# Feed-forward weights and residual of a hybrid decoder trunk: the fourth block split on the engines, output tiles added to the residual in DRAM by transfer

## The chip, the cores and the metric

The kernel runs on one core of one Trainium2 chip. The metric is the device time of one execution in microseconds (us), and the time of a kernel is the median of its runs. The engines are named as in the profile: PE (TensorE's matmuls), PEld (its weight loads), DVE (VectorE), ACT (ScalarE), POOL (GpSimd) and SP (SyncE). GpSimd and SyncE do hardly anything here but issue transfers. A transfer issued on SyncE goes into one DMA queue, one issued on GpSimd into another; both are served by the same 16 DMA engines.

## The reference

A trunk of two layers, all in float32, with 512 tokens, a model width of 1024 and a hidden width of 2816. Each layer has a mixing part and a feed-forward part. Only the second one is touched:

```python
for i in range(DEPTH):                      # DEPTH = 2
    h = rmsnorm(x, norm_mix[i])
    ...
    x = x + merged @ w_mix_o[i]             # attention, convolution and state-space branches, gated
    h = rmsnorm(x, norm_ffn[i])
    gt, up = jnp.split(h @ w_ffn_in[i], 2, axis=-1)
    x = x + (jax.nn.silu(gt) * up) @ w_ffn_out[i]
return rmsnorm(x, norm_final)
```

## The kernel before

**Products of split numbers.** Data are kept transposed: 128 channels on the partitions, 512 tokens along the free axis, so that the residual is eight tiles of 128x512. TensorE multiplies in a reduced format, fp32r. Every operand is therefore kept as two tiles, hi (the value rounded to fp32r) and lo (what is left over, rounded too), and a product is three matmuls, hi by hi, hi by lo and lo by hi (`mm3`, L271; all its matmuls are at L275). Making a pair costs one copy on ScalarE for hi and one subtraction on VectorE for lo (`lo_of`, L189, whose instruction is at L190).

**The feed-forward part.** The hidden width is 22 tiles of 128, taken in five groups: tiles 0 to 5, 6 to 9, 10 to 13, 14 to 17 and 18 to 21. Tiles 0 to 5 are computed plainly. A tile from 6 on is a "pair tile": its gate and its up projection are treated as the two rows of a 2x2 block matrix and multiplied in seven products instead of eight (`seven_products`, L1130). Each product runs over four blocks of the inner width, with three 128x256 matmuls for each, so a pair tile has 84 matmuls. The seven products are gathered in the PSUM tiles pb, pc and pd; ScalarE copies parts of them into the SBUF tiles ga and ub in between (L1148 to L1155), and VectorE later finishes ga by adding pd (L1168 in a pair tile, L1187 in an output; all such additions are recorded at L363) and ub from pb (recorded at L367). This finishing is deferred: it is a generator that runs beside the products of the next tile. In a pair tile a Silu on ScalarE follows (L1169).

The output of the groups 6 to 9, 10 to 13 and 14 to 17 is made in seven products too (`out_pairs`, L1177, called in the loop below after the first pair tile of the group that follows). It goes through the eight residual tiles two by two, four steps of 42 matmuls, and adds each result onto the residual, which at that time lies in DRAM as `xkept`: for each tile, 128x512 numbers or 256 KB, SyncE loads the old value into a tile xs (L1184), VectorE adds ga or ub, and SyncE stores xs back (L1189 and L1193). So there are three such output groups in a layer, with eight loads and eight stores each. The loads of a step are issued one step ahead. After the last pair tile the residual is loaded once more (xres, L1250), and the last group's output, `pfo`, is added to it in SBUF.

**Weights of the pairs.** Every pair tile, and every two steps of an output group, takes one item of weights from a DRAM tensor `wsp`; there are 22 items in a layer. `fetch_chunk` (L168) issues an item's transfers on GpSimd's queue: r2 plainly (L175, 128x1024, 512 KB), h4 (L176, 128x512, 256 KB), a second block accumulated onto r2 (L177), and r1 (L178). An accumulating transfer reads what lies at its destination and writes the sum back. h4 is the fourth block of the matrix, which the transfer itself rounds to fp32r. `item_steps` (L201) then makes the seven operands: ScalarE writes -h4 into l4 (L195) and GpSimd issues a transfer that accumulates the block onto it (L196), which leaves the block's low part; h1 is copied from r1, r3 is added up from r2 and r1 on VectorE (L225 and L227), and h2, l1, h3, l2, l3 follow in this order. `feed`, called after each of the seven products, advances this by two steps. Two items are fetched ahead.

**Buffers and order.** r1, r2 and r3 share 5 buffers (NPART), the hi tiles of 128x1024 share 5, the lo tiles 5, and all tiles of 128x512 (xs, ga, ub, h4, l4, the operands) share 58. Each engine works its instructions off in one fixed order. That order is chosen when the kernel is built, by a scheduler that models durations, except in one part of the kernel's beginning that is ordered by hand. The same holds for GpSimd's and SyncE's lists of transfers: a transfer that has to wait for a buffer or a result holds up all that stand behind it in that list.

Of the kernel before, what the change touches and what calls it, by code (L numbers as in the profile page):

```python
# [9 lines left out]
F32 = mybir.dt.float32  # L10
F32R = mybir.dt.float32r
I32 = mybir.dt.int32
AF = mybir.ActivationFunctionType
ALU = mybir.AluOpType
PSUM = bass.MemoryType.PSUM

P = 128
D = 1024
S = 512
DEPTH = 2  # L20
KT = D // P
# [59 lines left out]
def hybrid_kernel(ctx, tc, xin, wst, wsp, vec, ssp, ssb, sbt, cst, out):  # L81
    nc = tc.nc
    V, A, T = nc.vector, nc.scalar, nc.tensor
# [13 lines left out]
    def u2(shape, dt=F32, name="u2"):  # L97
        return up.tile(shape, dt, tag="u2", bufs=NU2, name=name)
# [58 lines left out]
    raws = []  # L157

    def wraw(name, dt=F32):
        return wp.tile([P, 1024], dt, tag="part", bufs=NPART, name=name)  # L160

    def whi(name="whi", dt=F32R):
        return wp.tile([P, 1024], dt, tag="whi", bufs=NHI, name=name)

    def wlo(name="wlo", dt=F32R):
        return wp.tile([P, 1024], dt, tag="wlo", bufs=NLO, name=name)

    def fetch_chunk(queue=nc.sync, parts=1):  # L168
        i, n, *half = items[loaded[0]]
        loaded[0] += 1  # L170
        if n is None:

            r1, r2, h4 = wraw("r1"), wraw("r2"), u2([P, S], F32R, "h4")
            n = half[0]
            nc.gpsimd.dma_start(r2[:, : 2 * n], wsp[i, :, 1024 : 1024 + 2 * n])  # L175
            nc.gpsimd.dma_start(h4[:, :n], wsp[i, :, 2048 : 2048 + n])  # L176
            nc.gpsimd.dma_start(r2[:, : 2 * n], wsp[i, :, 2048 : 2048 + 2 * n], accum_op=ALU.add)  # L177
            nc.gpsimd.dma_start(r1[:, : 2 * n], wsp[i, :, 0 : 2 * n])  # L178
            raws.append((i, n, r1, r2, h4))
            return None  # L180
        raw = wp.tile([P, 1024], F32, tag="raw", bufs=NRAW, name="raw")
        n //= parts
        cuts = [slice(j * n, (j + 1) * n) for j in range(parts)]
        for c in cuts:
            dma = queue.dma_start(raw[:, c], wst[i, :, c])
        raws.append((raw, cuts))
        return dma

    def lo_of(lo, raw, hi):  # L189
        V.tensor_tensor(out=lo, in0=raw, in1=hi.bitcast(F32), op=ALU.subtract)  # L190
        return lo

    def rest_of(lo, hi, src):

        A.activation(lo, hi.bitcast(F32), AF.Copy, scale=-1.0)  # L195
        nc.gpsimd.dma_start(lo, src, accum_op=ALU.add)  # L196
        return lo

    fetched = [0]
# [1 line left out]
    def item_steps():  # L201
        if not raws:
            fetch_chunk()
        got = raws.pop(0)
        while sum(1 + (len(x) > 3) for x in raws) < fetched[0] and loaded[0] < len(items):
            fetch_chunk()
        if len(got) == 2:
            raw, cuts = got
            hi, lo = whi(), wlo()
            for c in cuts:  # L210
                A.copy(hi[:, c], raw[:, c])  # L211
                yield
                lo_of(lo[:, c], raw[:, c], hi[:, c])
                yield
            ready.append((cuts[-1].stop * 3 // P, (hi, lo)))
            return
        i, n, r1, r2, h4 = got
        a, b, ab = slice(0, n), slice(n, 2 * n), slice(0, 2 * n)
        l4 = u2([P, S], F32R, "l4")
        rest_of(l4[:, a], h4[:, a], wsp[i, :, 2048 : 2048 + n])  # L220
        yield
        h1 = whi("h1")
        A.copy(h1[:, ab], r1[:, ab])
        r3 = wraw("r3")
        V.tensor_tensor(out=r3[:, a], in0=r2[:, a], in1=r1[:, a], op=ALU.add)  # L225
        yield
        V.tensor_tensor(out=r3[:, b], in0=r3[:, a], in1=r1[:, b], op=ALU.add)  # L227
        yield
        h2, l1 = whi("h2"), wlo("l1")
        A.copy(h2[:, ab], r2[:, ab])  # L230
        lo_of(l1[:, ab], r1[:, ab], h1[:, ab])
        yield
        h3, l2 = whi("h3"), wlo("l2")
        A.copy(h3[:, ab], r3[:, ab])  # L234
        lo_of(l2[:, ab], r2[:, ab], h2[:, ab])
        yield
        l3 = wlo("l3")
        lo_of(l3[:, ab], r3[:, ab], h3[:, ab])
        part = lambda h, l, c: (h[:, c], l[:, c])
        ready.append((7 * n // P * 3 // 2,  # L240
            dict(a11=part(h1, l1, a), a12=part(h1, l1, b), s1=part(h2, l2, a), s3=part(h2, l2, b),
                 s2=part(h3, l3, a), s4=part(h3, l3, b), a22=part(h4, l4, a))
        ))
        yield

    def load_chunk():
        for _ in item_steps():
            pass
# [3 lines left out]
    def feed(steps=1000):  # L252

        while steps and sum(n for n, _ in ready) < AHEAD and (feeding or raws or loaded[0] < len(items)):
            if not feeding:
                feeding.append(item_steps())
            if next(feeding[0], "end") == "end":
                feeding.pop()
            steps -= 1

    def take():
        while not ready:
            feed(1)
        return ready.pop(0)[1]
# [97 lines left out]
    def tt(out, a, b, op):  # L362
        V.tensor_tensor(out=out, in0=a, in1=b, op=op)  # L363
        return out

    def stt(out, a, s, b, o0, o1):
        V.scalar_tensor_tensor(out=out, in0=a, scalar=s, in1=b, op0=o0, op1=o1)  # L367
        return out
# [10 lines left out]
    for k in range(KT):  # L379
# [3 lines left out]
        if k == 3:  # L383
            fetch_chunk()
    xg = []
    first = item_steps()
    with tc.manual_schedule(engines={mybir.EngineType.DVE, mybir.EngineType.Activation}):
        for k in range(KT):
# [63 lines left out]
    def first_products(ssum):  # L452

        u = u_products(ssum)
        pq, ws = [mmps([P, S], "pqb") for _ in range(NB - 1)], [chunk()]
        q_products(pq, ws, [0], range(NB - 1))
        u = u_evacuated(*u)
        ws.append(chunk())
        q_products(pq, ws, [1], range(NB - 1))
        pq.append(mmps([P, S], "pqb"))  # L460
        q_products(pq, ws, [0, 1], [NB - 1])
        return u + ((pq, ws),)
# [5 lines left out]
    uts, rcol, rb, r2, qprod = first_products(ssum)  # L468
# [16 lines left out]
    def tiny(dt=F32, shape=(P, LQ)):  # L485
        _n[0] += 1
        return cp.tile(list(shape), dt, name=f"ssm_c{_n[0]}")
# [73 lines left out]
    for lo_, hi_, by in ((2, 3, 1), (3, 5, 2)):  # L561
        n = hi_ - lo_
        dst = [pw[:, i, lo_:hi_] for i in range(2)]
        src = [pw[:, i, lo_ - by : hi_ - by] for i in range(2)]
        m = [pw[:, i, by : by + 1].to_broadcast([P, n, LQ]) for i in range(2)]
# [27 lines left out]
    r4 = er  # L593
    for _ in range(2):
        cph, sph = double_angle(cph, sph)
        r4 = tt(tiny(), r4, r4, ALU.mult)
# [324 lines left out]
    for l in range(DEPTH):  # L921
        if l > 0:
            uts, rcol, rb, r2, qprod = first_products(ssum)
# [204 lines left out]
        flat = lambda x: x.rearrange("p a c -> p (a c)")  # L1128
# [34 lines left out]
        def pair_tile(made, beside):  # L1163

            ga, ub, pd, pb = seven_products(ops, beside, take())

            def evacuated():
                tt(ga, ga, pd, ALU.add)  # L1168
                A.activation(ga, ga, AF.Silu)  # L1169
                yield  # L1170
                stt(ub, pb, -1.0, ub, ALU.mult, ALU.subtract)
                yield
                yield from made(flat(ga), flat(ub))

            return [evacuated()]

        def out_pairs(ops, beside):  # L1177

            xs = []

            def fetch_x(m):
                xs.append([u2([P, S], F32, "xs") for _ in range(2)])
                for j in range(2):
                    nc.sync.dma_start(xs[-1][j], xkept[:, m + j])  # L1184

            def evacuated(m, x, ga, ub, pd, pb):
                tt(ga, ga, pd, ALU.add)  # L1187
                tt(x[0], x[0], flat(ga), ALU.add)
                nc.sync.dma_start(xkept[:, m], x[0])  # L1189
                yield  # L1190
                stt(ub, pb, -1.0, ub, ALU.mult, ALU.subtract)
                tt(x[1], x[1], flat(ub), ALU.add)
                nc.sync.dma_start(xkept[:, m + 1], x[1])  # L1193
                yield

            fetch_x(0)
            for m in range(0, KT, 2):
                if m + 2 < KT:
                    fetch_x(m + 2)
                if m % 4 == 0:  # L1200
                    w = take()
                got = seven_products(ops, beside, w, m % 4)
                beside = [evacuated(m, xs.pop(0), *got)]
            return beside

        xkept = dr.tile([P, KT, S], F32, name=f"xkept{l}")
        nonlocal_rb = []
        beside, due = [], []
        for gi, (f0, f1) in enumerate(FGROUPS):
# [14 lines left out]
            for f in range(f0, f1):  # L1224
# [12 lines left out]
                beside = pair_tile(made, beside)  # L1237
                if due:
                    beside = out_pairs(due.pop(), beside)
# [6 lines left out]
            beside = []  # L1246
# [238 lines left out]
```

## Time and profile before

| | |
|---|---|
| median of 3 runs | 1584.59 us (1581.96 to 1584.94) |
| profiled execution | 1581.27 us, its span 1579.3 us |
| granted TensorE clock, mean over the span | 0.994 |

Busy time of the engines in the four stages of the program (PE, PEld, DVE, ACT and POOL with their instruction counts, then the granted clock, the DMA engines' mean busy share and GB/s):

```profile
0.00:503.00 503.00, 494.74 (x2467) 406.55 (x2468) 374.62 (x894) 211.63 (x387) 61.73 (x122) 1.00 0.38 117
503.00:800.00 297.00, 291.52 (x2150) 278.36 (x2150) 228.03 (x309) 164.05 (x279) 70.53 (x104) 1.00 0.85 235
800.00:1277.00 477.00, 475.57 (x2391) 390.80 (x2390) 342.75 (x750) 197.28 (x366) 60.43 (x116) 1.00 0.36 108
1277.00:1579.30 302.30, 283.03 (x2201) 275.44 (x2199) 227.30 (x342) 158.10 (x283) 75.41 (x111) 0.97 0.79 217
```

The first and the third stage are the mixing parts and the plain tiles of the two layers. The second and the fourth hold the pair tiles and the output groups, and the fourth also the end of the program. The DMA engines work more than twice as hard in the second and fourth stage as in the others. The transfers that the change touches are these (queue, count, size of one, median us from its issue to its landing):

```profile
r<-wsp POOLq DMA_DIRECT2D x132, 512.0 KB, 6.5
...
xs<-xkept SPq DMA_DIRECT2D x48, 256.0 KB, 6.1
xkept<-xs SPq DMA_DIRECT2D x48, 256.0 KB, 6.4
h<-wsp POOLq DMA_DIRECT2D x44, 256.0 KB, 5.8
l<-wsp POOLq DMA_DIRECT2D x44, 256.0 KB, 7.3
```

A row of a timeline gives the start in us, the duration, engine, line, operation, output and inputs with their shapes, a count, and in brackets how long the engine sat idle before it and what ended that. A row of the list of waits gives the waiting tile, what it waited for, the total, how often, and the longest.

### The profile page before, as it was taken

To read this page: it belongs to the slowest core of one execution; us is meant where nothing else is said; L and a number is where in the kernel's file an instruction comes from. 1 tells how busy PE (TensorE), PEld (TensorE's weight loads), DVE (VectorE), ACT (ScalarE), POOL (GpSimd) and SP (SyncE) were. 2 spreads that over 40 slices of the span, in tenths; PEclk is the share of its full clock that TensorE was granted. 3 is DMA by queue.
4 is the path that set the end of the run, shared out by engine and by line. 5 is a ranking of instruction groups with operands and counts; after the bars stand their busy time and mean duration, and the time that the engine had idled before them with its cause. 6 is when DMAs were issued, how large, how long until landed. Compare 5 with 4: busy or idle time off the path is not lost.

```text
span 1579.3 us, 24934 instructions
## 1 busy us (share of the span) xinstructions
PE 1544.9 (98%) x9204; PEld 1351.1 (86%) x9204; DVE 1172.7 (74%) x2294; ACT 731.1 (46%) x1314; POOL 268.1 (17%) x451
## 2 busy tenths in 40 slices
PE   9899999999999999999999999999999999999996
PEld 7777878888888999999888778788888889999995
DVE  7985869766667687988768666896476756888876
ACT  4345533334444365665524555233444434665652
POOL 0301023210001133332020012122100012333201
PEclk9999999999999999999999999999999999999998
DMA  6423235432533899989543233345234258999952
GB/s 224 124 82 81 78 94 136 137 107 89 179 100 96 227 223 273 280 235 255 188 140 114 74 84 89 115 111 157 73 126 160 84 161 215 252 253 287 271 166 89
DMA packets 108026, 245.89 MB, mean 156 GB/s; under 512 B 23072, under 2 KB 28480, under 8 KB 107904
## 3 DMA queue, kind: packets, MB, share of 16 engines
q1 hardware_dynamic: 69280, 144.77, 28.0%
q0 software_dynamic: 38336, 99.00, 25.7%
q8 instruction: 73, 1.20, 0.3%
q10 hardware_dynamic: 288, 0.52, 0.1%
q14 instruction: 49, 0.40, 0.1%
HBM read 218.01 MB, written 22.02 MB: 152 GB/s over the span
## 4 chain that ended last, share of the span: by engine, by line
PE 82%; DMA 6%; DVE 5%; issue 4%; ACT 1%; POOL 1%; SPq 0%; DVEq 0%; POOLq 0%; ACTq 0%
PE pg L275 17%; PE pc L275 11%; PE py L275 8%; PE pd L275 7%; PE pfo L275 7%; PE pb L275 7%; PE px L275 6%; PE pfu L275 4%; PE pfg L275 4%; DMA r<-wsp 3%; DMA xkept<-xs 2%; PE pu L275 1%; PE pqb L275 1%; PE pz L275 1%; PE pS L857 1%
## 5 line engine op out<-in xcount | busy, mean ns | idle before, releaser
L211 ACT CAST whi<-raw 128x1024 fp32r<-128x1024 f32 (+2 forms) x214 | 195.4, 917 | 434.2 <-PE pg L275 114.2
L190 DVE TENSOR_TENSOR wlo<-raw,whi 128x1024 fp32r<-128x1024 f32 (+2 forms) x214 | 225.4, 1055 | 93.9 <-ACT whi L211 82.3
L190 DVE TENSOR_TENSOR l<-r,h 128x1024 fp32r<-128x1024 f32 x132 | 160.4, 1218 | 12.5 <-ACT h L234 10.5
L275 PE MATMUL pg<-hi,whi 128*128 128x512 f32 x384 | 152.2, 396 | 0.0
L275 PE MATMUL pg<-hi,wlo 128*128 128x512 f32 x384 | 150.4, 392 | 0.0
L275 PE MATMUL pg<-lo,whi 128*128 128x512 f32 x384 | 150.0, 391 | 0.0
L275 PE MATMUL pd<-hi,l 128*128 128x256 f32 x528 | 148.1, 283 | 1.7 <-DVE l L190 1.7
L275 PE MATMUL pd<-hi,h 128*128 128x256 f32 x528 | 148.3, 283 | 0.0
L275 PE MATMUL pd<-lo,h 128*128 128x256 f32 x528 | 147.9, 283 | 0.0
L275 PE MATMUL pb<-hi,h 128*128 128x256 f32 x352 | 100.5, 285 | 6.9 <-ACT ga L1148 5.5
L275 PEld LDWEIGHTS pd<-hi,l 128*128 128x128 f32 x528 | 100.9, 192 | 2.1 <-DVE l L190 2.1
L275 PEld LDWEIGHTS pd<-lo,h 128*128 128x128 f32 x528 | 100.9, 192 | 0.0
L275 PEld LDWEIGHTS pd<-hi,h 128*128 128x128 f32 x528 | 100.9, 192 | 0.0
L275 PE MATMUL pb<-hi,l 128*128 128x256 f32 x352 | 99.6, 283 | 0.0
L275 PE MATMUL pb<-lo,h 128*128 128x256 f32 x352 | 99.6, 283 | 0.0
L176 POOL DMA_DIRECT2D h<-wsp x44 | 29.6, 674 | 362.4 <-PE pfu L275 330.6
L275 PEld LDWEIGHTS pg<-hi,whi 128*128 128x128 f32 x384 | 72.2, 188 | 15.8 <-DVE at_nm L357 0.4
L275 PEld LDWEIGHTS pg<-hi,wlo 128*128 128x128 f32 x384 | 72.1, 188 | 15.2
L275 PEld LDWEIGHTS pg<-lo,whi 128*128 128x128 f32 x384 | 72.2, 188 | 14.3
L275 PE MATMUL pc<-hi,whi 128*128 128x512 f32 x192 | 77.9, 406 | 2.4 <-ACT qr L820 2.4
L275 PE MATMUL pc<-lo,whi 128*128 128x512 f32 x192 | 76.5, 399 | 0.0
L275 PE MATMUL pc<-hi,wlo 128*128 128x512 f32 x192 | 76.3, 397 | 0.0
(302 smaller groups left out, 4327.6 us busy)
## 6 DMA issues: line engine op xcount, KB each, us to landing
raw<-wst SPq DMA_DIRECT2D x140, 512.0 KB, 3.5
r<-wsp POOLq DMA_DIRECT2D x132, 512.0 KB, 6.5
raw<-wst SPq DMA_DIRECT2D x56, 256.0 KB, 2.7
xs<-xkept SPq DMA_DIRECT2D x48, 256.0 KB, 6.1
xkept<-xs SPq DMA_DIRECT2D x48, 256.0 KB, 6.4
h<-wsp POOLq DMA_DIRECT2D x44, 256.0 KB, 5.8
l<-wsp POOLq DMA_DIRECT2D x44, 256.0 KB, 7.3
raw<-wst SPq DMA_DIRECT2D x16, 384.0 KB, 3.0
```

The costliest lines, as they stand in the source:

```text
L176: nc.gpsimd.dma_start(h4[:, :n], wsp[i, :, 2048 : 2048 + n])
L190: V.tensor_tensor(out=lo, in0=raw, in1=hi.bitcast(F32), op=ALU.subtract)
L211: A.copy(hi[:, c], raw[:, c])
L275: T.matmul(o, a, b, start=start and i == 0, stop=stop and i == 2, skip_group_check=more)
L857: T.matmul(pS[par][:, hp, keys], qt[a][rows, 2 * k + hp], kt[b][rows, k, keys], start=i == 0, stop=i == 2,)
```

## The change

Two edits in the feed-forward part, both for the pair tiles and the three output groups of each layer.

*The fourth block of each item.* It is now loaded unrounded, into a float32 tile r4, as the last of the item's four transfers instead of the second. Its high and low part are made as those of the other blocks are: a copy on ScalarE (h4) and a subtraction on VectorE (l4), as a step of their own just before l3. The scaling by -1 on ScalarE and the accumulating transfer on GpSimd's queue go away. Over the kernel these are 44 transfers fewer on GpSimd, 44 copies for 44 scalings on ScalarE, and 44 subtractions of 128x512 more on VectorE.

*The residual of the output groups.* The finished ga or ub goes by an accumulating transfer on GpSimd's queue straight onto its tile of `xkept` in DRAM. The tiles xs, their 48 loads and 48 stores on SyncE's queue and the 48 additions on VectorE go away; 48 accumulating transfers of 256 KB come onto GpSimd's queue.

```diff
-            r1, r2, h4 = wraw("r1"), wraw("r2"), u2([P, S], F32R, "h4")
+            r1, r2, r4 = wraw("r1"), wraw("r2"), u2([P, S], F32, "r4")
             n = half[0]
             nc.gpsimd.dma_start(r2[:, : 2 * n], wsp[i, :, 1024 : 1024 + 2 * n])
-            nc.gpsimd.dma_start(h4[:, :n], wsp[i, :, 2048 : 2048 + n])
             nc.gpsimd.dma_start(r2[:, : 2 * n], wsp[i, :, 2048 : 2048 + 2 * n], accum_op=ALU.add)
             nc.gpsimd.dma_start(r1[:, : 2 * n], wsp[i, :, 0 : 2 * n])
-            raws.append((i, n, r1, r2, h4))
+            nc.gpsimd.dma_start(r4[:, :n], wsp[i, :, 2048 : 2048 + n])
+            raws.append((i, n, r1, r2, r4))
...
-    def rest_of(lo, hi, src):
-
-        A.activation(lo, hi.bitcast(F32), AF.Copy, scale=-1.0)
-        nc.gpsimd.dma_start(lo, src, accum_op=ALU.add)
-        return lo
...
-        l4 = u2([P, S], F32R, "l4")
-        rest_of(l4[:, a], h4[:, a], wsp[i, :, 2048 : 2048 + n])
-        yield
         h1 = whi("h1")
...
+        yield
+        h4, l4 = u2([P, S], F32R, "h4"), u2([P, S], F32R, "l4")
+        A.copy(h4[:, a], r4[:, a])
+        lo_of(l4[:, a], r4[:, a], h4[:, a])
         yield
         l3 = wlo("l3")
...
         def out_pairs(ops, beside):
 
-            xs = []
-
-            def fetch_x(m):
-                xs.append([u2([P, S], F32, "xs") for _ in range(2)])
-                for j in range(2):
-                    nc.sync.dma_start(xs[-1][j], xkept[:, m + j])
-
-            def evacuated(m, x, ga, ub, pd, pb):
+            def evacuated(m, ga, ub, pd, pb):
                 tt(ga, ga, pd, ALU.add)
-                tt(x[0], x[0], flat(ga), ALU.add)
-                nc.sync.dma_start(xkept[:, m], x[0])
+                nc.gpsimd.dma_start(xkept[:, m], flat(ga), accum_op=ALU.add)
                 yield
                 stt(ub, pb, -1.0, ub, ALU.mult, ALU.subtract)
-                tt(x[1], x[1], flat(ub), ALU.add)
-                nc.sync.dma_start(xkept[:, m + 1], x[1])
+                nc.gpsimd.dma_start(xkept[:, m + 1], flat(ub), accum_op=ALU.add)
                 yield
 
-            fetch_x(0)
             for m in range(0, KT, 2):
-                if m + 2 < KT:
-                    fetch_x(m + 2)
                 if m % 4 == 0:
                     w = take()
                 got = seven_products(ops, beside, w, m % 4)
-                beside = [evacuated(m, xs.pop(0), *got)]
+                beside = [evacuated(m, *got)]
             return beside
```

Lines behind the edits move up by 5 to 17. The names of tiles in the orders below end in a running number.

On GpSimd's list, at the first output group of layer 0, before (L175 to L178 are the loads of an item, L196 is the accumulation onto l4):

```order
L175 DMA r2_6006<-wsp 128x1024
L178 DMA r1_6005<-wsp 128x1024
L176 DMA h4_6152<-wsp 128x512
L196 DMA l4_6157<-wsp 128x512
L177 DMA r2_6006<-wsp 128x1024
L176 DMA h4_6275<-wsp 128x512
L196 DMA l4_6280<-wsp 128x512
L175 DMA r2_6151<-wsp 128x1024
L178 DMA r1_6150<-wsp 128x1024
L177 DMA r2_6151<-wsp 128x1024
```

At the same place after the change (now L175 is r2, L176 its accumulation, L177 r1 and L178 r4; L1176 and L1179 are the accumulations onto the residual):

```order
L176 DMA r2_5995<-wsp 128x1024
L1176 DMA xkept0_4365<-ga_5984 128x512
L1179 DMA xkept0_4365<-ub_5985 128x512
L1176 DMA xkept0_4365<-ga_6065 128x512
L175 DMA r2_6137<-wsp 128x1024
L178 DMA r4_6261<-wsp 128x512
L1179 DMA xkept0_4365<-ub_6066 128x512
L177 DMA r1_6136<-wsp 128x1024
L176 DMA r2_6137<-wsp 128x1024
```

The h4 and l4 transfers are gone from between the loads, and the outputs of the group stand between them in their place, each behind the instruction that makes its ga or ub.

On VectorE, inside a pair tile of layer 0, before:

```order
L363 TENSOR_TENSOR ga_5433<-ga_5433,pd_5432 128x512
L190 TENSOR_TENSOR l1_5492<-r1_5327,h1_5473 128x1024
L367 SCALAR_TENSOR_TENSOR ub_5434<-pb_5430,ub_5434 128x512
L190 TENSOR_TENSOR l2_5496<-r2_5328,h2_5491 128x1024
L363 TENSOR_TENSOR ga_5433<-ga_5433,ub_5434 128x512
L190 TENSOR_TENSOR l3_5512<-r3_5475,h3_5495 128x1024
```

and after:

```order
L358 TENSOR_TENSOR ga_5437<-ga_5437,pd_5436 128x512
L190 TENSOR_TENSOR l1_5480<-r1_5330,h1_5460 128x1024
L362 SCALAR_TENSOR_TENSOR ub_5438<-pb_5434,ub_5438 128x512
L190 TENSOR_TENSOR l2_5497<-r2_5331,h2_5479 128x1024
L358 TENSOR_TENSOR ga_5437<-ga_5437,ub_5438 128x512
L190 TENSOR_TENSOR l4_5624<-r4_5455,h4_5623 128x512
L190 TENSOR_TENSOR l3_5517<-r3_5462,h3_5496 128x1024
```

The only difference is the new subtraction for l4, ahead of that for l3.

On VectorE, at the end of the last pair tile of layer 1 (wlo and raw belong to the plain weights of the output that follows, lo and hi to the last hidden operand), before:

```order
L363 TENSOR_TENSOR ga_15978<-ga_15978,pd_15977 128x512
L367 SCALAR_TENSOR_TENSOR ub_15979<-pb_15975,ub_15979 128x512
L190 TENSOR_TENSOR wlo_16146<-raw_15994,whi_16145 128x1024
L190 TENSOR_TENSOR wlo_16184<-raw_16106,whi_16183 128x1024
L363 TENSOR_TENSOR ga_15978<-ga_15978,ub_15979 128x512
L290 TENSOR_TENSOR lo_16087<-ga_15978,hi_16086 128x512
```

and after:

```order
L358 TENSOR_TENSOR ga_15878<-ga_15878,pd_15877 128x512
L190 TENSOR_TENSOR wlo_16046<-raw_15894,whi_16045 128x1024
L362 SCALAR_TENSOR_TENSOR ub_15879<-pb_15875,ub_15879 128x512
L190 TENSOR_TENSOR wlo_16084<-raw_16006,whi_16083 128x1024
L358 TENSOR_TENSOR ga_15878<-ga_15878,ub_15879 128x512
L285 TENSOR_TENSOR lo_15987<-ga_15878,hi_15986 128x512
```

One of the two wlo subtractions has moved up between ga and ub. On TensorE the last products of that tile change place with it: before, the last 24 matmuls are 6 into pb, 12 into pd and 6 into pb, and 18 of the output `pfo` follow; now they are 12 into pd and 12 into pb, and 23 of the output follow.

More of the change, by code (lines that the diff above doesn't have):

```diff
@@ L216, in item_steps @@
             return
-        i, n, r1, r2, h4 = got
+        i, n, r1, r2, r4 = got
         a, b, ab = slice(0, n), slice(n, 2 * n), slice(0, 2 * n)
-        l4 = u2([P, S], F32R, "l4")
-        rest_of(l4[:, a], h4[:, a], wsp[i, :, 2048 : 2048 + n])
-        yield
         h1 = whi("h1")
```

## The prediction

> **What bounds the kernel now.** I read the page first, then TensorE's list of waits over the two stretches that the change touches (the pair tiles and out groups of layer 0, 535.9 to 768 us, and of layer 1, 1309 to 1545 us).
>
> ```profile
> span 1579.3 us, 24934 instructions
> PE 1544.9 (98%) x9204; PEld 1351.1 (86%) x9204; DVE 1172.7 (74%) x2294; ACT 731.1 (46%) x1314; POOL 268.1 (17%) x451
> PE pb L275 <- ACT ga L1148: 3.5, 3, 2.2
> PE pd L275 <- DVE l L190: 0.8, 1, 0.8
> PE pb L275 <- ACT ga L1153: 0.6, 1, 0.6
> ...
> PE pfo L275 <- ACT hi L289: 2.2, 1, 2.2
> PE pb L275 <- ACT ga L1148: 2.0, 3, 0.9
> PE pd L275 <- DVE l L190: 0.8, 1, 0.8
> PE pb L275 <- ACT ga L1153: 0.8, 1, 0.8
> ```
>
> TensorE is busy 98% of the span. The change removes no matmul, so it can only win or lose TensorE waits. Columns: total, times, longest. Layer 0 has 4.9 us in five waits, layer 1 5.8 us in six: 10.7 us in eleven. Each costs more than its row says, as the longest chain in layer 0's first out group shows:
>
> ```profile
> 610.93 1.22 DVE L190 TENSOR_TENSOR l<-r,h 128x1024 fp32r<-128x1024 f32 x1
> 612.56 0.85 POOL L196 DMA_DIRECT2D l<-wsp  x1 [2.27 <-ACT l L195]
> 613.10 0.88 POOL L175 DMA_DIRECT2D r<-wsp  x1
> 614.17 0.55 POOL L178 DMA_DIRECT2D r<-wsp  x1 [0.20 <-issue]
> 622.48 0.88 POOL L177 DMA_DIRECT2D r<-wsp  x1 [7.75 <-DVE ga L363]
> 628.21 0.69 DVE L225 TENSOR_TENSOR r<-r,r 128x512 f32<-128x512 f32 x1 [4.76 <-DMA r<-wsp]
> 630.26 0.63 ACT L1169 ACTIVATE ga<-ga 128x512 f32<-128x512 f32 x1 [3.95 <-DVE ga L363]
> 630.82 0.28 PE L275 MATMUL pd<-hi,l 128*128 128x256 f32 x1
> 632.15 0.39 PE L275 MATMUL pb<-hi,h 128*128 128x256 f32 x1 [1.05 <-ACT ga L1148]
> 632.37 0.28 PE L275 MATMUL pb<-lo,h 128*128 128x256 f32 x1
> 537.50 2.88 PE pd L275 x24
> ```
>
> A matmul of this form takes 2.88 / 24 = 0.12 us. From 630.82 to 632.37 two of them took 1.55 us, 1.31 too long, where the row shows 1.05: 0.26 us more per wait. The eleven are worth 10.7 + 11 x 0.26 = **13.6 us**: the ceiling.
>
> The chain reads backwards: TensorE waits for ScalarE's copy of ga, which is queued behind a Silu that waits for VectorE, which sits 4.76 us at L225 because r2's accumulation (L177) is late. L177 was issued at 622.48, when the plain load of r2 (L175, 613.10) had landed after 9 us. Why 9 us, the transfer windows show (columns: stretch, its length, busy time of PE, PEld, DVE, ACT, POOL, then clock, DMA share, GB/s):
>
> ```profile
> 547.60:577.80 30.20, 30.20 (x254) 30.20 (x254) 22.87 (x31) 18.10 (x30) 9.00 (x14) 1.00 0.92 215
> 598.00:618.10 20.10, 20.10 (x169) 20.10 (x169) 18.01 (x23) 13.58 (x25) 7.31 (x11) 1.00 1.06 290
> 618.10:658.40 40.30, 39.25 (x327) 39.05 (x326) 34.45 (x51) 23.99 (x43) 13.03 (x19) 1.00 0.92 256
> 543.00:546.00 3.00, 3.00 (x28) 3.00 (x27) 0.94 (x2) 1.71 (x3) 1.35 (x2) 1.00 1.00 162
> 608.00:610.00 2.00, 2.00 (x19) 2.00 (x18) 1.67 (x4) 1.01 (x1) 1.15 (x2) 1.00 1.06 400
> 621.50:624.00 2.50, 2.50 (x24) 2.50 (x23) 1.95 (x3) 0.90 (x3) 1.52 (x3) 1.00 0.05 18
> ```
>
> In the out group (598 to 618) the DMA engines are full (share 1.06), and they fall silent at 621.5, just when L177 could go: the transfers, not an engine, hold the chain. At a share of about 1 an accumulating transfer alone (L177 in 543 to 546) moves 162 GB/s, plain ones (608 to 610) 400. So 256 KB cost the full set of engines **x = 0.66 us plain, y = 1.6 us accumulating**. Test: an item of weights is now 5x + 3y = 8.1 us, an out group's residual 16x = 10.6; a period of one out group and four pair tiles (60.4 us, six items) asks 6 x 8.1 + 10.6 = 59.2, and the rows give 20.1 x 1.06 + 40.3 x 0.92 = 58.4.
>
> **The change part by part.**
>
> *Weights.* Every item loses l4's accumulation: 5x + 2y = 6.5 us. GpSimd loses one issue in five. ScalarE is even (44 copies for 44 scalings of the same shape). VectorE gains 44 subtractions of 128x512, which before does not have at L190; the nearest row is the first of these:
>
> ```profile
> L290 DVE TENSOR_TENSOR lo<-t,hi 128x512 fp32r<-128x512 f32 x12 | 8.2, 681 | 0.0
> L225 DVE TENSOR_TENSOR r<-r,r 128x512 f32<-128x512 f32 x20 | 13.8, 690 | 19.1 <-DMA r<-wsp 18.1 <-DVE l L190 0.5 <-DVE b L363 0.3
> L363 DVE TENSOR_TENSOR xs<-xs,ga 128x512 f32<-128x512 f32 x12 | 8.2, 688 | 0.2
> L363 DVE TENSOR_TENSOR xs<-xs,ub 128x512 f32<-128x512 f32 x12 | 8.2, 684 | 0.1
> ```
>
> 22 x 0.68 = 15.0 us more on VectorE in a layer, against 16.4 us of xs additions that go. But the additions go in the out groups and the subtractions come everywhere: from 618 to 658 VectorE rises from 34.5 to 34.5 + 4 x 0.68 = 37.2 of 40.3 us. What hides them is the 19.1 us that it sat before L225 in that layer. Cost zero; if the cover went, up to 0.68 us in each tile that is already full.
>
> *Residual.* 48 loads and 48 stores on SyncE's queue become 48 accumulating transfers on GpSimd's, whose destination is DRAM. No row shows that. Below, y: it reads two streams and writes one as L177 does. From the other side, stores to DRAM are no dearer than loads from it here (the fastest store landed in 2.0 us, the fastest load in 3.0):
>
> ```profile
> L1193 SPq DMA_DIRECT2D xkept<-xs x24: 319/320/840, 598.7 to 1518.9; - x24
> DMA to landing us min/median/max: 2.0/6.6/7.6
> ...
> L1184 SPq DMA_DIRECT2D xs<-xkept x48: 319/320/1601, 576.4 to 1500.2; - x48
> DMA to landing us min/median/max: 3.0/6.1/7.8
> ```
>
> So the bounds are x (0.66) and, with the dearest ratio that the rows show (y/x = 2.4) applied once more, 3.9 us. I take z = y = 1.6, the row nearest in kind. [...]
>
> The period then asks 6 x 6.5 + 8 x 1.6 = 51.8 of 60.5 us: 98% becomes 86%. It stays within 60.5 up to **z = 2.7 us**.
>
> *The chain again.* On GpSimd's queue the eight accumulations stand between weight loads, each waiting for VectorE's ga or ub; behind them wait r4, r1 and both steps of r2 of the next items. The last three rows of before's queue up to L177 are those of the trace above; L175 there waited behind L196 (issued 612.56), which is gone. In the changed kernel L175 goes when its buffer is free, about 611.5 (VectorE's subtraction that frees it, first row of that trace, ended at 612.1, with additions of 0.68 us ahead of it that go). In the ring ahead of it: the previous r2 accumulation (an estimate: from about 606, 2y), then three outputs (3z), so 606 + 3.2 + 4.8 + 1.3 for itself = 615.3, and some 2 us to land: **617.3 instead of 622.4**. L177's successor and the Silu move by the same 5 us; TensorE's wait was 1.05.
>
> So the sum, by waits:
> - Late r2, both layers (two ga waits in layer 0, two in layer 1: 4.8 us of the rows' 5.5, the other 0.7 being waits for a buffer that a store held): -(4.8 + 4 x 0.26) = -5.8.
> - Buffer waits: unchanged, since ScalarE's copies now wait for buffers that an accumulation reads instead.
> - pd <- l, 0.84 each: two xs additions ahead of that subtraction go (1.2 us), one l4 comes (0.6). -0.6 each, -1.2.
> - ga L1153, 0.6 and 0.8, at the end of the third out group; again a late r2 behind 4.7 us of idle VectorE. -(1.4 + 0.5) = -1.9.
> - hi L289, 2.2, at the end of layer 1:
>
> ```profile
> 1537.92 0.69 DVE L363 TENSOR_TENSOR ga<-ga,pd 128x512 f32<-128x512 f32 x1 [3.42 <-PE pd L275]
> 1538.63 0.69 DVE L367 SCALAR_TENSOR_TENSOR ub<-pb,ub 128x512 f32<-128x512 f32 x1
> 1539.24 2.35 DVE L190 TENSOR_TENSOR wlo<-raw,whi 128x1024 fp32r<-128x1024 f32 x2
> 1542.90 0.82 PE L275 MATMUL pfo<-hi,whi 128*128 128x256 f32 x4 [2.19 <-ACT hi L289]
> ```
>
>  The new order puts one wlo between ga and ub, and on TensorE pd ahead of pb, so ga runs under pb's last 12 matmuls (1.44 us). -1.3.
> - New: in each of six out groups one restart (0.26) for a copy that meets an accumulation: +1.5.
>
> Together -10.2 + 1.5 = **-8.7 us**. The profiled execution took 1581.27 us (span 1579.3), 3.3 below the median of the three runs, 1584.59. 1581.27 - 8.7 = 1572.6; moved to the median, **1576**.
>
> **Rivals.**
> 1. *r2 stays late.* All outputs now share one queue with the weights. For: three outputs stand ahead of r2's load; if each takes 3z = 7.5 us instead of 4.8 (z = 2.5), the load lands at 620 and only half the late-r2 waits shrink. -2.9 - 1.2 - 0.9 - 1.3 + 3 (twice as many new waits) = -3.3: 1581, about the border of no change. Against: the period still has 8 us to spare. [...]
> 2. *Accumulating into DRAM is dear: slower.* From z = 2.7 the transfers become the bound. At z = 3.2 a period asks 39 + 25.6 = 64.6, 4.1 us too much; six groups, 25 us, and none of the gains: 1584.6 + 25 = 1610. At 3.9 it is 9.7 x 6 = 58, so 1643. Against: the plain stores above.
> 3. *VectorE becomes the bound.* In two tiles of each four, operands are made and VectorE had no idle (10.1 of 10.1 us). 12 such tiles x 0.68 = 8.2 us more, with half the gains: 1584.6 + 8.2 - 4.4 = 1588. Against: it started those stretches late because of r2.
>
> **How the numbers follow.** Forecast 0.60, rival 1 0.20, rival 2 0.13, rival 3 0.07. 0.2%, 3.2 us, is about what a measurement of this kernel can tell from no change. Faster by more: the forecast and a fifth of rival 1, 0.64; same: the rest of rival 1 and a little of 3, 0.18; slower 0.18. The forecast's own range is 1571 (all 13.6 gone) to 1580; with rivals 1 and 3 the range is 1571 to 1592. Outside lies rival 2 (0.13) and a few hundredths.
>
> **What would show it.** Right: layer 0's idle before L225's line falls from 19.1 us to under 10; the DMA share of the first out group ends below 1 soon after 615; r2's plain load lands in under 7 us there; TensorE's waits in the two stretches sum to under 5 us. The accumulations into DRAM, alone at a share of 1, move about 160 GB/s; under 100 would be rival 2. Rival 3 would show as pb or pd waits on VectorE from 570 to 592 and 634 to 658 us. I would be wrong from the start if the change moved rows before 500 us or in the tail after the last pair tile.

## The result, and the profile after

The changed kernel takes 1572.12 us (median of six runs, 1569.21 to 1575.32), against 1582.82 us for the kernel before (six runs, 1578.82 to 1584.94): a ratio of 0.9936, interval 0.9919 to 0.9953, or 7 to 13 us less. The forecast was 1576, in a range of 1571 to 1592. The profiled execution of the changed kernel, 1575.32 us, is the slowest of its six.

The page of the changed kernel, its span, the engines' totals and the two queues of transfers (packets, MB, share of the 16 engines' span), and then the list of TensorE's waits over the same stretches as before, with the end of layer 0 (768 to 812 us) between them:

```profile
span 1573.3 us, 24686 instructions
PE 1545.0 (98%) x9204; PEld 1351.4 (86%) x9204; DVE 1171.0 (74%) x2290; ACT 730.2 (46%) x1314; POOL 271.4 (17%) x455
q0 software_dynamic: 36096, 100.05, 27.2%
q1 hardware_dynamic: 55456, 119.60, 23.9%
```

```profile
PE pb L270 <- ACT ga L1143: 2.0, 2, 1.2
...
PE pfo L270 <- DVE xres L358: 1.9, 1, 1.9
...
PE pfo L270 <- ACT hi L284: 1.1, 1, 1.1
PE pb L270 <- ACT ga L1143: 0.8, 2, 0.6
```

TensorE is as busy as before. In the two stretches its eleven waits of 10.7 us have become five of 3.9 us: no wait for VectorE's l is left, and none for a buffer that a store held. A wait in the stretch between grew, from 0.5 to 1.9 us. That is the outcome the prediction summed up, but its main step is not there. These are VectorE's idle times before the first r3 addition in layer 0 (535 to 768 us; the column behind the second bar), and GpSimd's list at the first output group:

```profile
L216 DVE TENSOR_TENSOR r<-r,r 128x512 f32<-128x512 f32 x20 | 13.8, 688 | 17.1 <-DMA r<-wsp 15.2 <-issue 1.0 <-DVE l L190 0.7
```

```profile
609.47 0.86 POOL L176 DMA_DIRECT2D r<-wsp  x1 [4.20 <-DMA r<-wsp]
610.02 1.21 POOL L1176 DMA_DIRECT2D xkept<-ga  x1
610.57 1.53 POOL L1179 DMA_DIRECT2D xkept<-ub  x1
611.12 1.87 POOL L1176 DMA_DIRECT2D xkept<-ga  x1
611.69 1.86 POOL L175 DMA_DIRECT2D r<-wsp  x1
...
622.24 0.88 POOL L176 DMA_DIRECT2D r<-wsp  x1 [6.68 <-DMA r<-wsp]
```

VectorE still sat 17.1 us before that line (19.1 before), and r2's plain load (L175) was issued at 611.69, directly behind three outputs of the same queue, and landed at 622.24, where the prediction had 617.3. So r2 is late in the changed kernel too. The question for the experiments is what did remove the waits, and which of the two edits.

Profiled executions differ ahead of these stretches too: the first matmul of the pair tiles started at 535.91 us before and at 537.25 after, and in a second profile of the changed kernel (e0) at 539.81. Below, "length" is the time from that matmul to the end of the span: 1579.3 - 535.91 = 1043.4 before, 1573.3 - 537.25 = 1036.1 after, 7.3 us less.

### The profile page after: what moved, and what is told of

It reads as the page before. It is cut to its first block, busy times and chain, and to the rows that moved or that the text cites. A ratio compares the mean times of both kernels' runs of the same rounds, so it can differ in the third digit from the quotient of the medians.

```text
span 1573.3 us, 24686 instructions
## 1 busy us (share of the span) xinstructions
PE 1545.0 (98%) x9204; PEld 1351.4 (86%) x9204; DVE 1171.0 (74%) x2290; ACT 730.2 (46%) x1314; POOL 271.4 (17%) x455
## 4 chain that ended last, share of the span: by engine, by line
PE 85%; DMA 5%; DVE 4%; issue 3%; POOL 1%; ACT 1%; SPq 0%; DVEq 0%; POOLq 0%; ACTq 0%
PE pg L270 17%; PE pc L270 11%; PE py L270 8%; PE pd L270 7%; PE pb L270 7%; PE pfo L270 6%; PE px L270 6%; PE pfu L270 4%; PE pfg L270 4%; DMA r<-wsp 4%; PE pu L270 3%; PE pqb L270 2%; PE pz L270 1%; PE pS L852 1%; PE po L898 1%
## 5 line engine op out<-in xcount | busy, mean ns | idle before, releaser
L190 DVE TENSOR_TENSOR l<-r,h 128x1024 fp32r<-128x1024 f32 (+1 forms) x176 | 187.8, 1086 | 9.9 <-ACT h L214 4.2
L178 POOL DMA_DIRECT2D r<-wsp x44 | 34.2, 778 | 339.4 <-PE pfu L270 330.6
```

The costliest lines, as they stand in the source:

```text
L178: nc.gpsimd.dma_start(r4[:, :n], wsp[i, :, 2048 : 2048 + n])
```

## The experiments

**The first edit alone (e1).** out_pairs is that of before, with xs, its loads and its stores:

```diff
-                nc.gpsimd.dma_start(xkept[:, m], flat(ga), accum_op=ALU.add)
+                tt(x[0], x[0], flat(ga), ALU.add)
+                nc.sync.dma_start(xkept[:, m], x[0])
...
```

> The first edit alone: the fourth block is loaded plainly and split by ScalarE and VectorE; the residual still goes through xs on SyncE's queue. Theory A (the transfer budget and r2's place behind other transfers make r2 late, and late r2 makes most of TensorE's waits): an item asks 6.5 us of the full set of DMA engines instead of 8.1, the period 49.6 of 60.4 us, and in its own ring r2's plain load has no accumulation onto l4 ahead of it; the load lands in 3 to 6 us in the first out group instead of 9, VectorE's idle before the first r3 addition in layer 0 falls from 19 us to under 12, the ga waits at the second pair tile of each period go, some 5 us, ratio about 0.997. The two pd<-l waits of 1.1 us each stay, since the xs additions ahead of that subtraction stay. Theory B (the gain of the whole change comes from the xs additions that leave VectorE): ratio 1.000 within 0.2%, or above it for the 44 subtractions that VectorE gains.

**The second edit alone (e2).** The kernel before with the new out_pairs; the fourth block still goes through `rest_of`:

> The second edit alone: outputs are accumulated onto the residual in DRAM; the fourth block still goes through the accumulation onto l4. Theory A (transfer budget): with z = 1.9 us for an accumulation into DRAM (the page of the changed kernel: software queue's share times span up by 22 us while 44 accumulations of 1.6 us went and 48 came), a period asks 6 x 8.1 + 8 x 1.9 = 64 us of 60.4, so it gets slower, by some 3.5 us in each of six groups where nothing else gives, 20 us at most, ratio 1.003 to 1.013. Theory B (VectorE's relief): faster by about what the whole change brought, ratio 0.993 to 0.996; the pd<-l waits are gone in either.

Measured: e1 1574.63 us, ratio 0.9936 (0.9923 to 0.9949); e2 1578.61 us, ratio 0.9969 (0.9954 to 0.9985); before in the same runs 1584.39. The rows before the first r3 addition in layer 0, of e1 and of e2:

```profile
L216 DVE TENSOR_TENSOR r<-r,r 128x512 f32<-128x512 f32 x20 | 13.7, 687 | 3.9 <-issue 2.5 <-DMA r<-wsp 1.3
```

```profile
L225 DVE TENSOR_TENSOR r<-r,r 128x512 f32<-128x512 f32 x20 | 13.8, 689 | 22.9 <-DMA r<-wsp 22.7
```

The first edit alone brings 10 us, more than either theory had allowed. VectorE's idle falls to 3.9 us, and none of the six waits behind late r2 is left in its list of TensorE's waits (layer 0, then layer 1, without two at the end of layer 1):

```profile
PE pb L270 <- ACT ga L1143: 2.1, 3, 1.4
...
PE pb L270 <- ACT ga L1143: 1.5, 3, 0.8
```

Two of its signs missed. r2's load in the first output group took 7.6 us (612.62 to 620.17), less than the 9.4 before but not the 3 to 6 expected, and the pd <- l waits, which should have stayed, are gone too. The idle is also no clean sign of late r2, since VectorE has some 15 us more to do in each layer here (the l4 subtractions, beside the xs additions that stay), and work fills idle time.

The second edit alone makes r2 no earlier (22.9 us of idle) and is faster all the same. Its list of TensorE's waits, layer 0 and then layer 1, shows why:

```profile
PE pb L275 <- ACT ga L1148: 3.1, 2, 1.6
...
PE pb L275 <- ACT ga L1148: 3.9, 2, 2.5
PE pfo L275 <- ACT hi L289: 0.9, 1, 0.9
```

The four waits behind late r2 grew from 4.8 to 7.0 us, but the two waits for l (0.8 each), the two for a held buffer and the two at L1153 are gone. The pages of these four kernels also give the price of a transfer, as the difference in a queue's share times span. GpSimd's queue with and without the outputs: 0.272 x 1573.3 - 0.220 x 1573.5 (e1) = 81.8 us for 48, z = 1.7 us; 0.306 x 1576.8 (e2) - 0.257 x 1579.3 = 76.6, z = 1.6. Both are near the 1.6 taken. With and without the accumulation onto l4: 59.7 us for 44, 1.36 us (before and e1), or 0.306 x 1576.8 - 0.272 x 1573.3 = 54.6, 1.24 us (e2 and the changed kernel), less than the 1.6 taken for y; these two also hold what h4's rounding load costs more or less than r4's plain one. None of these prices is fixed: the accumulations that e5 and e9 add below, also into DRAM, come out at 1.16 and 1.17 us by the same count (for e9 0.252 x 1577.4 - 0.220 x 1573.5 = 51.3 us for 44). Theory A of e2 started from z = 1.9, which had come out by keeping l4's accumulation at 1.6, and it said slower; that was wrong.

**Each output accumulated twice (e5)**, the second time onto a tensor that nothing reads:

```diff
                 nc.gpsimd.dma_start(xkept[:, m], flat(ga), accum_op=ALU.add)
+                nc.gpsimd.dma_start(twice[:, m], flat(ga), accum_op=ALU.add)
```

> The changed kernel with each of the 48 accumulations into DRAM issued a second time onto a second DRAM tensor that nothing reads. By the transfer budget with z = 1.9 us a period asks 6 x 6.5 + 16 x 1.9 = 69.4 of 60.4 us: 9 us in each of six groups, about 54 us more than the changed kernel; with z = 1.6 (taken in the prediction) 64.6, so 25 us more. If the accumulations cost no shared time (each waits only on its own latency), under 5 us more.

One run: 1607.79 us, span 1606.0, 32.7 more than the changed kernel's. The prediction's formula with a z of 1.65 gives 6 x 6.5 + 16 x 1.65 = 65.4 us for a period of 60.4, that is 5.0 x 6 = 30. That the two are so close is luck in part. TensorE's waits in the two stretches and between them sum to 27.8 us, 22 more than in the changed kernel; the other 10 are the clock, which fell to 0.50 behind five of these waits and lost 11.9 us, against 1.7. And by the queue's share times the added transfers cost 0.301 x 1606.0 - 0.272 x 1573.3 = 55.5 us for 48, 1.16 each, with which the formula gives 61.5 us and a loss of 6.5. So outputs in this queue can cost a lot, and r2 is later with them (20.1 us of VectorE's idle in layer 0, against 17.1 and 19.0 in two profiles of the changed kernel); that a period's transfers fill the engines is not shown by it.

**r2's plain load on the other queue (e3):**

```diff
-            nc.gpsimd.dma_start(r2[:, : 2 * n], wsp[i, :, 1024 : 1024 + 2 * n])
+            nc.sync.dma_start(r2[:, : 2 * n], wsp[i, :, 1024 : 1024 + 2 * n])
```

> The changed kernel with r2's plain load issued on SyncE's queue instead of GpSimd's; its accumulation stays on GpSimd's. Ring theory (r2's load takes 10.5 us at the first out group of the changed kernel because three accumulations into DRAM stand ahead of it in the same queue): the load lands in under 6 us, VectorE's idle before the first r3 addition in layer 0 falls from 17 us to under 8, the four ga waits left in the pair tiles (1.1, 1.4, 0.8 and 0.5 us with their restarts) mostly go, 2 to 3.5 us less than the changed kernel, ratio 0.991 to 0.993 against the kernel before. Bandwidth theory (the DMA engines are full there, whichever queue it comes from): landing and idle as in the changed kernel, ratio 0.9936 as there.

**The same edit in the kernel before (e10):**

> The kernel before with nothing changed but the queue of r2's plain load: SyncE's instead of GpSimd's. The DMA engines carry the same bytes by the same operations. Queue theory: r2's load no longer stands behind the accumulations onto l4, VectorE's idle before the first r3 addition in layer 0 falls from 19 us to under 12, and some of the late-r2 waits go: 3 to 5 us, ratio 0.997 to 0.998. Engine-time theory (a period's transfers fill the 16 engines): within 0.2% of the kernel before. Rival: on SyncE's queue the loads stand between the residual's loads and stores, each of which waits for VectorE, and r2 is as late or later: 1.000 or above.

Measured: e3 1570.22 us, ratio 0.9909 (0.9896 to 0.9922); e10 1583.12 us, ratio 1.0005 (0.9986 to 1.0023). The first output group in e3 (SyncE's row, then GpSimd's) and in e10:

```profile
610.96 0.33 SPq L175 DMA_DIRECT2D r<-wsp  x1
...
618.03 0.85 POOL L176 DMA_DIRECT2D r<-wsp  x1 [2.85 <-DMA r<-wsp]
```

```profile
612.89 1.50 SPq L1189 DMA_DIRECT2D xkept<-xs  x1
614.56 1.15 SPq L175 DMA_DIRECT2D r<-wsp  x1
...
623.30 0.83 POOL L177 DMA_DIRECT2D r<-wsp  x1 [6.72 <-DMA r<-wsp]
```

In e3 SyncE issues nothing but three of these loads from 600 to 622 us, and the load lands 7.1 us after its issue, where the changed kernel took 10.6 (611.69 to 622.24), while the same outputs are being accumulated. That is the ring theory's direction, though not its size (under 6 us): VectorE's idle falls from 17.1 to 11.3 us, not under 8. TensorE's four waits behind late r2, 2.8 us together, become two, 1.1 us together, and the kernel gains 1 to 2 us by the medians, which the intervals allow to be nothing. In e10 the queue holds the residual's stores, the load takes 8.7 us, and nothing is won. e10 went as its rival said; engine-time theory expected the same, so it does not part those two.

**The removed engine time given back, on SyncE's queue (e6), and on GpSimd's (e9).** Both start from e1. e6 stores two blocks of 256 KB per item, e9 accumulates one:

```diff
         lo_of(l4[:, a], r4[:, a], h4[:, a])
+        for src in (r4[:, a], h4[:, a].bitcast(F32)):
+            nc.sync.dma_start(dr.tile([P, S], F32, tag="spare", bufs=8, name="spare"), src)
```

```diff
         A.copy(h1[:, ab], r1[:, ab])
+        nc.gpsimd.dma_start(dr.tile([P, S], F32, tag="spare", bufs=8, name="spare")[:, a], h1[:, a].bitcast(F32), accum_op=ALU.add)
```

> The first edit alone (e1), with two plain stores of 256 KB per item (r4 and h4 to a DRAM tensor that nothing reads) on SyncE's queue: the DMA engines' time of the removed accumulations onto l4 (44 x 1.35 us by the pages of before and e1) is given back, but not their place in GpSimd's queue. If it was the engines' time that made r2 late, VectorE's idle before the first r3 addition in layer 0 goes from 3.9 us back towards 19, above 12, and the ratio to 0.998 or more. If it was the place in the queue, the idle stays under 8 us and the ratio within 0.2% of e1's 0.9936.

> The first edit alone (e1), with one accumulating transfer of 256 KB per item put back on GpSimd's queue (a block of h1 onto a DRAM tensor that nothing reads, behind the copy of h1, so that it waits for ScalarE as the accumulation onto l4 did); VectorE's order is e1's. Queue theory (what made r2 late is such a transfer among the weight loads of the same queue): VectorE's idle before the first r3 addition in layer 0 goes from 3.9 us to 10 or more, the wait behind it comes back, ratio 0.996 to 0.999. If e1's gain came from VectorE's new order, idle and ratio stay as in e1 (3.9 us, 0.9936).

Measured: e6 1579.96 us, ratio 0.9979 (0.9961 to 0.9998); e9 1583.51 us, ratio 1.0000 (0.9984 to 1.0015). Idle before the first r3 addition in layer 0, and GpSimd's rows of the same r2 as above, of e6 and of e9:

```profile
L216 DVE TENSOR_TENSOR r<-r,r 128x512 f32<-128x512 f32 x20 | 13.7, 687 | 3.5 <-DMA r<-wsp 3.4
...
613.17 0.54 POOL L175 DMA_DIRECT2D r<-wsp  x1 [2.29 <-DVE l L190]
620.18 0.87 POOL L176 DMA_DIRECT2D r<-wsp  x1 [4.74 <-DMA r<-wsp]
```

```profile
L217 DVE TENSOR_TENSOR r<-r,r 128x512 f32<-128x512 f32 x20 | 13.8, 688 | 12.6 <-DMA r<-wsp 8.7 <-issue 3.8
...
613.70 0.55 POOL L175 DMA_DIRECT2D r<-wsp  x1
...
620.46 0.87 POOL L215 DMA_DIRECT2D spare<-h  x1 [4.49 <-ACT ga L1144]
623.68 0.87 POOL L176 DMA_DIRECT2D r<-wsp  x1 [2.36 <-DMA r<-wsp]
```

The load takes 7.0 us in e6, with about as much engine time given back as was removed (0.319 x 1576.5 - 0.283 x 1573.5 = 57.6 us on SyncE's queue), against 9.4 in the kernel before (613.10 to 622.48); in e9 it takes 10.0. Side by side, with the landing counted from the first matmul of the pair tiles, the idle of layer 0 and the length as above, all in us:

| | r2's load, issue to landing | landing | VectorE's idle | length |
|---|---|---|---|---|
| before | 9.4 | 86.6 | 19.1 | 1043.4 |
| after | 10.6 | 85.0 | 17.1 | 1036.1 |
| e1, first edit | 7.6 | 83.6 | 3.9 | 1036.9 |
| e2, second edit | 10.1 | 86.1 | 22.9 | 1039.7 |
| e3, after, load on SyncE | 7.1 | 81.2 | 11.3 | 1031.5 |
| e6, e1 and stores on SyncE | 7.0 | 83.4 | 3.5 | 1039.7 |
| e9, e1 and accumulations on GpSimd | 10.0 | 86.0 | 12.6 | 1039.8 |
| e10, before, load on SyncE | 8.7 | 85.9 | 19.7 | 1044.3 |

So this load lands late where accumulating transfers share its queue (in e10, stores), and earlier where e1 takes them away, e3 takes it out of their queue, or e6 spends the same time on the other one. The time of the kernel does not follow that alone: e6 and e9 have the same length, and the intervals of their ratios overlap. In e9 the whole gain is gone by the ratio, but not by the mechanism expected: r2 landed as late as before, and of TensorE's six waits behind it only one came back, with 0.40 us (at 694.88). One reason is VectorE's order. In the kernel before, both r3 additions stand ahead of the one that adds pd to ga, which starts 1.3 us after the first of them (628.21 and 629.55). In e9:

```profile
629.43 0.69 DVE L217 TENSOR_TENSOR r<-r,r 128x512 f32<-128x512 f32 x1 [3.68 <-DMA r<-wsp]
630.04 0.68 DVE L359 TENSOR_TENSOR ga<-ga,pd 128x512 f32<-128x512 f32 x1
```

Here, as in e1, ga comes directly behind the first r3 addition, 0.6 us after it started. So the order that came with the first edit has a share in its gain, 0.7 us at such a place, and how the gain divides between r2's place and the order is not settled. e6 fits neither branch of its expectation, though: r2 stays in time, yet most of the ratio is lost. Its waits at the end of layer 0 and in both stretches show a part of that elsewhere:

```profile
PE pd L272 <- ACT ub L1148: 1.0, 1, 1.0
...
PE pfo L272 <- DVE xres L360: 3.0, 1, 3.0
...
PE pd L272 <- ACT ub L1148: 0.8, 1, 0.8
```

With the added stores on SyncE's queue TensorE waits 1.0 and 0.8 us for ub, which it does not in e1's lists, and 3.0 us for xres, where e1 has 1.4. e9's profile does not show its loss either: it is of the second fastest of its twelve executions, its length is 3 us over e1's, and its runs lie 9 above e1's. Of the other 6 us some 3 are the clock, by an estimate: (1 - mean granted clock) x span is 10.7 us on average in e9's runs and 7.6 in e1's. The rest has not been seen.

**The changed kernel again (e0), with the residual loads moved (e4), and with e3's edit too (e7):**

```diff
+                if f == NF - 1:
+                    xres = [u2([P, S], F32, "xres") for _ in range(KT)]
+                    for m in range(KT):
+                        nc.sync.dma_start(xres[m], xkept[:, m])
                 beside = pair_tile(made, beside)
...
-            if f0 > 0:
-                xres = [u2([P, S], F32, "xres") for _ in range(KT)]
-                for m in range(KT):
-                    nc.sync.dma_start(xres[m], xkept[:, m])
```

> The changed kernel itself again, beside the next three on one chip, so that they can be set against it: ratio 0.992 to 0.995 against the kernel before. Its first profile, 1575.3 us, was the slowest of six runs; in it TensorE waited 2.3 us for xres at the first layer's end and then ran at half clock for 3.7 us. If the clock drop depends on when the wait falls, a second profile may lack it and be 1.5 to 2 us shorter.

> The changed kernel with the eight residual loads of the last group issued ahead of the last pair tile instead of behind it; TensorE's order is the same. If the loads' lateness makes the wait of the first output tile for xres (2.3 us at layer 0 in the changed kernel's profile, 0.8 before), that wait goes to under 0.5 us and with it the half clock behind it: 1.5 to 4 us less than the changed kernel, ratio near 0.992. Rival: the loads only change places with the weight tiles raw on SyncE's queue, and TensorE waits as long for those: within 1 us of the changed kernel.

> The changed kernel with both: r2's plain load on SyncE's queue (e3, 0.9909) and the early xres loads (e4). If the two waits are independent, the gains add: 2 us below e3 where the xres wait of 1.9 us in e3's profile goes, ratio 0.989 to 0.991. If xres's lateness only shows because TensorE came earlier, or the loads now collide with r2's on SyncE's queue, the same as e3.

Measured, on one chip beside 1583.0 us for the kernel before: e0 1571.44 us, ratio 0.9911 (0.9892 to 0.9930); e4 1569.44, 0.9902 (0.9883 to 0.9921); e7 1568.91, 0.9900 (0.9881 to 0.9919). e4's list of waits from 768 to 812 us is empty, as its theory said; the gain, 2 us, is inside the intervals, but e4's five runs end at 1570.86 and e0's six reach 1575.69. e7 adds nothing to e4 that could be measured: with xres early, r2's queue is worth 0.5 us by the medians. These are the fastest versions tried. e0's profile confirms that r2 is late in the changed kernel (its load took 11.2 us, VectorE's idle is 19.0). The half clock behind xres is missing in it, as was allowed for; its span is 0.4 us longer all the same, since it lost 2.6 us ahead of the pair tiles.

## Why the prediction was right, point by point

The size came out right, from terms that were off in both directions; to that extent it was luck. For r2 rival 1's picture held, and other waits that the prediction had left standing went instead. Waits are summed as in the prediction, each with 0.26 us for its restart, from the profiled executions before and after.

- **Late r2** (the four waits at L1148 and the two at L1153): 6.2 us + 6 x 0.26 = 7.8 before, 2.8 + 4 x 0.26 = 3.9 after, so -3.9, where the prediction took all of it (-5.8 and -1.9). The step that failed is the arrival of r2's load: it came at 622.2, where the ring's sum had 617.3. Most of that lies in the sum's first term, not in z: it let the previous accumulation of r2 start at about 606 us, and that one was issued at 609.47, having waited for its own late load. Counted from the first matmul of the pair tiles, the load came 1.6 us earlier than before and not 5. The three outputs ahead of it are rival 1's picture, and it cost about what rival 1 allowed ("only half the late-r2 waits shrink"), though at a z of 1.65 and not 2.5. In e1 these waits are gone, with r2's load 3.0 us earlier and VectorE's new order; in e2, where outputs and accumulations onto l4 share the queue, the load lands at 86.1 us and four of the waits stay.
- **pd <- l**: -2.2 (two waits of 0.84 + 0.26) against -1.2. The waits are gone altogether, and so they are in e2, where no l4 subtraction came, which fits that the xs additions that left VectorE were worth more than the prediction credited. In e1, where the additions stayed, TensorE stands near the same two places for ga instead (1.4 and 0.8 us).
- **Buffer waits**: 0.23 and 0.43, with restarts 1.2, predicted to stay, are gone. That points at the stores: e2 has none, and e1, which kept the stores, has waits for ga in its output groups, 2.1 and 1.5 us in six (the two just named among them).
- **New restarts**: +1.5 predicted, none found.
- **hi at the end of layer 1**: the wait fell from 2.2 to 1.1, -1.1 against -1.3, by the step named there. A further gain was not foreseen: the half clock that followed the longer wait is gone (below).
- **xres at the end of layer 0**: not foreseen. The loads went out at 767.71 us and the first addition onto xres could start at 773.80; TensorE came sooner than before, its wait grew by 1.4 us, and a half clock followed (SyncE's row and VectorE's, then the stretches):

```profile
767.71 5.73 SPq L1233 DMA_DIRECT2D xres<-xkept  x8
...
773.80 2.08 DVE L358 TENSOR_TENSOR xres<-xres,pfo 128x512 f32<-128x512 f32 x3 [4.58 <-DMA xres<-xkept]
```

```profile
774.00:776.00 2.00, 1.46 (x5) 1.17 (x6) 1.97 (x4) 1.48 (x2) 0.00 (x0) 0.81 1.05 405
776.00:778.00 2.00, 2.00 (x7) 1.51 (x6) 2.00 (x3) 2.00 (x5) 0.00 (x0) 0.50 1.04 382
778.00:780.00 2.00, 2.00 (x9) 1.65 (x8) 2.00 (x4) 2.00 (x4) 0.00 (x0) 0.83 0.97 305
```

By the clock column (third from the end) these three stretches lost 2 x (0.19 + 0.50 + 0.17) = 1.7 us. At the end of layer 1 the kernel before had lost 2 x (0.15 + 0.50 + 0.21) = 1.7 us in the same way:

```profile
1542.00:1544.00 2.00, 1.10 (x5) 0.91 (x6) 0.89 (x2) 0.62 (x1) 0.00 (x0) 0.85 0.84 325
1544.00:1546.00 2.00, 2.00 (x11) 2.00 (x11) 1.52 (x4) 1.06 (x3) 0.00 (x0) 0.50 0.07 27
1546.00:1548.00 2.00, 2.00 (x16) 2.00 (x16) 0.78 (x3) 0.60 (x2) 0.00 (x0) 0.79 0.04 8
```

Together -3.9 - 2.2 - 1.2 - 1.1 - 1.7 + 1.4 + 1.7 = -7.0, against 7.3 less in length. The second profile of the changed kernel (e0) has a length of 1573.7 - 539.81 = 1033.9, 9.5 less than before, and no half clock behind xres; that is closer to the medians' 10.7.

- **The budget of a period** was the wrong instrument for r2. By it the changed kernel had 8 us to spare, and r2 came late all the same; e2 asks 6 x 8.1 + 8 x 1.65 = 61.8 of 60.4 us and should have lost 8 us, or just fill the period with l4's accumulation at 1.36, and it won 5. Its y was read off 543 to 546 us as from one accumulating transfer alone, but three more transfers had been issued by 543.10. When r2's load lands goes with which transfers stand ahead of it in its own queue during the output group (the table above).
- **Rival 2** needed z above 2.7; the counts give 1.16 to 1.7, and from 611 to 613 us, with outputs just issued, the engines moved 156 GB/s at a share of 0.98, where under 100 was named as its sign. That accumulating into DRAM takes more of the engines' time than accumulating onto SBUF (1.24 to 1.36) these counts do not show. **Rival 3** needed waits on VectorE in the full tiles; there are none. The signs named in advance for r2 (idle under 10 us, landing in under 7 us, a share below 1 soon after 615 us: it stayed at 1.03 or more until 623) all failed, and the one for the sum (under 5 us of waits) held: 3.9.
- **Which edit?** First alone 0.9936, second alone 0.9969, both 0.9936 and 0.9911 in two sets. The first brings most of it; the second adds 0 to 4 us by these ratios, 2 to 3 by the medians (1574.63 against 1572.12 and 1571.44), at the edge of what can be told.

## What to carry to other kernels

Ask of a late load what stands ahead of it in its own queue at that moment, and not only how full the engines are over a period: with one accumulating transfer per item in its queue r2's load landed 2.4 us later than without (e9 against e1), with the same engine time in the other queue no later (e6). But do not price the kernel by that load alone: both additions cost time, 10 us and 7 by the ratios, and the profiles show 3 us for each. Moving the load to a queue that carries stores won nothing (e10: 8.7 us against 9.4, ratio 1.0005). When a change moves traffic into the queue of the loads that the chain hangs on, expect it to give back part of what it wins (here r2's load took 10.6 us behind the outputs and 7.1 on the other queue); and when a stage gets shorter, look at the loads that the next stage starts with, since they may have been only just in time (here the wait for xres grew from 0.5 to 1.9 us). And set two profiles against each other from a common event, not from the start of the program: r2's load looks as late after as before (622.2 and 622.5 us), and is 1.6 us earlier.

## What the runs showed of the hardware

A short wait of TensorE can cost twice. After the wait of 2.2 us that ended at 1542.9 us in the kernel before, and after that of 1.9 us at 774.5 in the changed one, the granted clock fell to 0.50 for some 3.4 us, 1.7 us lost each time; after one of equal length at 695 us in the kernel before it did not:

```profile
692.00:694.00 2.00, 0.90 (x8) 0.69 (x6) 2.00 (x3) 0.78 (x2) 0.37 (x1) 1.00 1.06 319
694.00:696.00 2.00, 0.89 (x7) 0.89 (x8) 2.00 (x4) 2.00 (x4) 1.05 (x2) 1.00 0.73 109
696.00:698.00 2.00, 2.00 (x19) 2.00 (x19) 2.00 (x4) 1.47 (x5) 0.54 (x1) 1.00 1.02 184
```

The other profiles bear that out, for TensorE's waits in the two stretches and at the end of layer 0. Of ten waits from 1.9 to 3.0 us, six were followed by the half clock (1.92 us after, 2.19 before, 2.55 in e2, 3.00 in e6, 1.95 in e9, 2.73 in e5) and four were not (2.21 before, 2.36 in e9, 2.88 and 2.19 in e10). No single wait from 1.3 to 1.9 us was; in e1 two of 1.0 and 0.6 us shortly after each other were. All four from 3.8 us up were (e5). Each time the clock stood at 0.50 for 3.4 us, 1.7 us lost, and behind two of the four longest for 6.8 us, 3.4 us lost.

So whether a wait of 2 to 3 us draws the half clock is not settled by its length; what does settle it, these profiles do not show. The drop is one source of the spread between executions of the same kernel, 1.7 us here: of two profiles of the changed kernel one had it behind xres, after a wait of 1.92 us, and the other, after one of 1.7 (e0), not.
